# Weight splits of the next stage tied behind the norm's reciprocal root, and more slots for the squares, in a two-layer trunk

## The chip, the cores and the metric

One core of one Trainium2 chip runs the whole program. The metric is the device time of one execution in microseconds (us), taken as the median of several runs. The profile is of one execution of its own.

## The reference

A sequence of 512 tokens with 16 learned tokens ahead of it (528 rows of 1024 features) goes through an input norm and two layers. All of it is in fp32. Cut to what matters here:

```python
for l in range(DEPTH):                       # DEPTH = 2
    h = layer_norm(DEEPNORM_ALPHA * h + 0.5 * swiglu_ffn(h, ffn1_w13[l], ffn1_w2[l]), ln_g[l, 0], ln_b[l, 0])
    mix = token_mix(h, w_in[l], ...)         # pooled, convolved and retention groups, one projection in, one out
    h = layer_norm(DEEPNORM_ALPHA * h + mix, ln_g[l, 1], ln_b[l, 1])
    h = layer_norm(DEEPNORM_ALPHA * h + 0.5 * swiglu_ffn(h, ffn2_w13[l], ffn2_w2[l]), ln_g[l, 2], ln_b[l, 2])
return h[:, N_META:]

def swiglu_ffn(x, w13, w2):
    a, u = jnp.split(x @ w13, 2, axis=-1)
    return (jax.nn.silu(a) * u) @ w2
```

`layer_norm` takes the mean and the variance over the 1024 features, and multiplies by the reciprocal root of the variance.

## The kernel before

**Stages.** The stages follow each other as f0a, m0, f0b, f1a, m1, f1b: ffn, mixer, ffn of layer 0, then of layer 1. After each of the first five stands a norm, after the last another form of it. So there are five places where a norm of this kind leads over to the first products of the next stage: f0a to m0, m0 to f0b, f0b to f1a, f1a to m1, m1 to f1b.

**Tiles.** Features lie on the partitions: the activations are eight tiles (m = 0 to 7) of 128 features, in two halves s of the tokens, 264 columns each. A matmul in full precision is three products of rounded parts (`mm3`, L130): high by high, low by high, high by low. So each operand is split in two: `weights()` (L86) has SP load a weight of 128x1024 into a "raw" tile (4 buffers), ScalarE casts it to its high part (L91), and VectorE subtracts that in two pieces of 512 columns to get the low part (L94).

**The norm.** `center` (L273) adds up the tiles and takes their mean by a matmul with ones (L283). VectorE subtracts the mean from each tile (L289), and ScalarE squares each (L291) into tiles q0 to q7 of the tag "q", which has 4 buffers. POOL adds q1 to q3 onto q0 and VectorE adds q5 to q7 onto q4 (both L296); VectorE joins the two sums (L298). `inv_var` (L182) sums the squares per token by small matmuls (L189), then a chain of eleven tiny VectorE operations on 88x3 elements (`inv_root`, L161 to L172) makes the reciprocal root, and a last one sets it on a diagonal (L192, the tile dg). Its instruction is kept in `rooted`. `inv_spread` (L201) spreads the diagonal over the partitions by a matmul, and `norm_apply` (L304) scales each tile (L308) and splits it into its x parts, high (L312, L315 on ScalarE) and low (even m on VectorE, L318 or L320; odd m on POOL, L313).

**Order around the norm.** `normed` (L337) issues the last step of the stage for the first half, that half's statistics, then the second half's steps for the same tiles, and the second half's statistics. The roots of the halves are `rooted["first"]` and `rooted["second"]`. A scheduler of the language orders each engine's instructions by its own estimate of when they are ready; `tc.issue_after(ins)` makes what is traced in its block follow `ins` on the engine of `ins`, here VectorE, and on no other.

**The next stage's first weights.** In an ffn, `hidden_part` (L488) takes three units in the plain way (0, 1 and 21); units 0 and 1 have two weights each, 21 one. In the mixer, the loop at L580 loads four weights for the "u" group (w0, w2, then w1, w3) and two for "xp" (w4, w5). Of these, only unit 21's splits are tied, behind the second root. Later ffn weights are sums of blocks, split by other functions (L431).

Of the kernel before, what the change touches and what calls it, by code (L numbers as in the profile page):

```python
# [40 lines left out]
PACE = (4, 3, 3, 2, 0)  # L41

ON_POOL = ("f0a_0", "f0a_1", "f0a_21")
LATE, LATE_W, LATE_B = 3, 2, 2

HM = NM // 2
NT = 256 + HM
# [11 lines left out]
def trunk(ctx, tc, a):  # L59
# [16 lines left out]
    def raw(r):  # L76
        return r.bitcast(F32)
# [5 lines left out]
        return vec[lo:hi, j : j + 1]  # L83


    def weights(src, n, name, e=nc.vector):  # L86
        w = wp.tile([P, 1024], F32, tag="raw", name=f"{name}_r", bufs=RAW)
        hi = wp.tile([P, 1024], F32R, tag="hi", name=f"{name}_h", bufs=WB)
        lo = wp.tile([P, 1024], F32R, tag="lo", name=f"{name}_l", bufs=WB)
        nc.sync.dma_start(out=w[:, :n], in_=src)  # L90
        nc.scalar.copy(out=hi[:, :n], in_=w[:, :n])  # L91
        for c in range(0, n, 512):
            sl = slice(c, min(c + 512, n))
            e.tensor_tensor(out=lo[:, sl], in0=w[:, sl], in1=raw(hi[:, sl]), op=ALU.subtract)  # L94
        return hi, lo

    def weights_wide(src, n, name):
# [175 lines left out]
    def center(tiles, n, width, name):  # L273

        s = tiles[0]
        if len(tiles) > 1:
            s = t(f"{name}_s", "s")
            nc.gpsimd.tensor_tensor(out=s[:, :n], in0=tiles[0][:, :n], in1=tiles[1][:, :n], op=ALU.add)  # L278
            for i, y in enumerate(tiles[2:]):
                e = nc.vector if i == len(tiles) - 3 else nc.gpsimd  # L280
                e.tensor_tensor(out=s[:, :n], in0=s[:, :n], in1=y[:, :n], op=ALU.add)  # L281
        mean = stat(f"{name}_mean")
        nc.tensor.matmul(mean[:, :n], lhsT=ones[width], rhs=s[:, :n], start=True, stop=True)  # L283

# [12 lines left out]
        if early:
            nc.vector.tensor_tensor(out=ss[0][:, :n], in0=ss[0][:, :n], in1=ss[1][:, :n], op=ALU.add)  # L298
        return inv_spread(inv_var(ss[0], n, width, name), n, name)
# [188 lines left out]
    def hidden_part(part, src, ns, name, between={}):  # L488
        hid, w = {}, {}
        plain = PARTS[part][: AHEAD if part == 0 else 0]  # L490
        for u, s in in_two(plain, AHEAD, between):
            if s == 0:
                i = plain.index(u)
                late = "first" in rooted and i >= LATE_W
                with tc.issue_after(rooted["second" if i >= LATE_B else "first"]) if late else nullcontext():
                    w[u] = unit_weights(u, src, f"{name}_{u}")
                hid[u] = []
            hid[u].append(hidden(u, w[u], s, ns[s], f"{name}_{u}"))
        if part == 0:
            summed[name] = sums(ns[0], name)  # L500
        for u in PARTS[part][len(plain) :]:
            with tc.issue_after(rooted["second"]) if plain and "second" in rooted else nullcontext():
                wu = sum_weights(src["p"][u], f"{name}_{u}")
            hid[u] = hidden_by_sums(wu, summed[name], ns[0], f"{name}_{u}")
        return hid
# [60 lines left out]
    def mixer(l, name):  # L566
# [13 lines left out]
        for (kind, c), s in in_two([("u", 0), ("u", 1), ("xp", 0), ("xp", 1)], 3):  # L580
            n = ns[s]
            if s == 0:
                tiles = (c, 2 + c) if kind == "u" else (4 + c,)
                ws[kind, c] = [weights(w_in[i], 1024, f"{name}w{i}") for i in tiles]
                p_ = pad if kind == "u" else ppad
                seq[kind, c] = wide(f"{name}{kind}{c}")[:, : p_ + L]
                nc.gpsimd.memset(seq[kind, c][:, :p_], 0.0)  # L587
            ps = project(ws[kind, c], s, n, f"{name}p{kind}{c}{s}")
            x_ = seq[kind, c]
            if kind == "u":  # L590
                sg = t(f"{name}sg{c}{s}", "g")
# [482 lines left out]
```

## Time and profile before

| | us |
|---|---|
| median of 3 runs (lowest, highest) | 1979.4 (1978.49, 1981.81) |
| the profiled execution, own time | 1979.3 |
| its span | 1977.5 |
| mean granted clock of TensorE | 0.99 |

The profile's rows use PE for TensorE's matmuls, DVE for VectorE, ACT for ScalarE, POOL for GpSimd and SP for the queue that loads weights. Numbers of buffers and halves are left out of names, so `f0a_ln_q` is any of the squares of the norm behind f0a. A row of a timeline has its start in us from the span's start, its length, the engine, the line and operation, what it writes and reads, the count, and in brackets how long the engine stood idle before it and what ended that. Lengths of one engine's instructions overlap a little, so the step from one start to the next is what an instruction costs in a row of them.

### The profile page before, as it was taken

Reading aid. Unit: us, or ns where it says so; the run is one execution under the profiler, and the core shown is the slowest. Engines: PE = TensorE matmul, PEld = TensorE weight load, DVE = VectorE, ACT = ScalarE, POOL = GpSimd, SP = SyncE. Lnnn points to the kernel's source line nnn. Section 1 sums busy time; section 2 is a strip of 40 time slices with the busy share of each in tenths; the row PEclk is TensorE's granted clock in tenths of the full one; section 3 lists DMA queues with packets and bytes.
Section 4 is the critical chain, followed back from the end, with each engine's and each line's share of the span. In section 5 each row is a group of like instructions: output and inputs, shape, how many; then the busy total and the mean of one; then the engine's idle time right before and its main releaser. Section 6 shows DMA issues by size and latency. Waiting matters only on the chain.

```text
span 1977.5 us, 36739 instructions
## 1 busy us (share of the span) xinstructions
PE 1912.4 (97%) x14423; PEld 1826.3 (92%) x14423; DVE 1548.9 (78%) x3466; ACT 920.1 (47%) x1845; POOL 215.0 (11%) x283
## 2 busy tenths in 40 slices
PE   7999999999999999999999999999999999999996
PEld 6999999997899899999989999998889998999995
DVE  7788778689767977788697787787897697877787
ACT  5454446443333644454464554464343265544451
POOL 4000000442003000000120000005320130000001
PEclk9999999999999999999999999999999999999998
DMA  4422323322112233323213323332131213323321
GB/s 143 129 86 97 116 88 104 100 76 85 63 34 75 64 98 108 97 89 107 95 54 111 101 89 107 97 118 75 65 104 54 65 44 118 107 86 107 107 97 43
DMA packets 61069, 177.98 MB, mean 90 GB/s; under 512 B 6976, under 2 KB 10944, under 8 KB 60896
## 3 DMA queue, kind: packets, MB, share of 16 engines
q1 hardware_dynamic: 59744, 174.59, 27.8%
q8 instruction: 113, 1.85, 0.4%
q10 hardware_dynamic: 1152, 1.05, 0.2%
q14 instruction: 60, 0.49, 0.1%
HBM read 173.52 MB, written 2.10 MB: 89 GB/s over the span
## 4 chain that ended last, share of the span: by engine, by line
PE 79%; DVE 12%; POOL 3%; issue 3%; ACT 2%; DMA 0%; SPq 0%; DVEq 0%; POOLq 0%; ACTq 0%
PE f0a_y L134 2%; PE f0a_y L133 2%; PE f1bo L890 2%; PE f1bo L888 2%; PE f0a_y L135 2%; PE f1bo L889 2%; PE f0b_y L134 2%; PE f1a_y L134 2%; PE f0b_y L133 2%; PE f0b_y L135 2%; PE f1a_y L135 2%; PE f1a_y L133 2%; DVE m0y L610 1%; DVE m1y L610 1%; PE m0sc L719 1%
## 5 line engine op out<-in xcount | busy, mean ns | idle before, releaser
L610 DVE SCALAR_TENSOR_TENSOR m1y<-m1u,vec,m1y 128x528 f32<-128x528 f32 x60 | 46.1, 801 | 0.0
L91 ACT CAST f0a_o_h<-f0a_o_r 128x512 fp32r<-128x512 f32 (+1 forms) x37 | 23.5, 635 | 48.4 <-PE f0a_y L134 29.5
L610 DVE SCALAR_TENSOR_TENSOR m0y<-m0u,vec,m0y 128x528 f32<-128x528 f32 x60 | 45.9, 801 | 0.0
L91 ACT CAST f1a_o_h<-f1a_o_r 128x512 fp32r<-128x512 f32 (+1 forms) x37 | 23.6, 637 | 48.0 <-PE f1a_y L134 29.0
L91 ACT CAST f0b_o_h<-f0b_o_r 128x512 fp32r<-128x512 f32 (+1 forms) x37 | 23.5, 636 | 47.6 <-PE f0b_y L134 29.3
L335 DVE TENSOR_TENSOR x<-x,f0a_y 128x264 f32<-128x264 f32 x64 | 27.1, 425 | 23.3 <-PE f0a_y L135 23.1
L335 DVE TENSOR_TENSOR h<-h,f0b_y 128x264 f32<-128x264 f32 x64 | 27.1, 425 | 23.2 <-PE f0b_y L135 23.1
L335 DVE TENSOR_TENSOR h<-h,f1a_y 128x264 f32<-128x264 f32 x64 | 27.1, 424 | 23.1 <-PE f1a_y L135 23.0
L94 DVE TENSOR_TENSOR f1bw_l<-f1bw_r,f1bw_h 128x512 fp32r<-128x512 f32 x42 | 27.7, 688 | 17.6 <-ACT f1bw_h L91 17.0
L949 POOL TENSOR_TENSOR yt<-yt,g_last 128x256 f32<-128x256 f32 x4 | 3.0, 740 | 337.2 <-ACT yt L948 337.2
L94 DVE TENSOR_TENSOR f0a_o_l<-f0a_o_r,f0a_o_h 128x512 fp32r<-128x512 f32 (+1 forms) x42 | 26.6, 642 | 13.4 <-ACT f0a_o_h L91 11.3
L94 DVE TENSOR_TENSOR f1a_o_l<-f1a_o_r,f1a_o_h 128x512 fp32r<-128x512 f32 (+1 forms) x42 | 26.7, 642 | 13.4 <-ACT f1a_o_h L91 11.4
L94 DVE TENSOR_TENSOR f0b_o_l<-f0b_o_r,f0b_o_h 128x512 fp32r<-128x512 f32 (+1 forms) x42 | 26.7, 642 | 12.6 <-ACT f0b_o_h L91 10.4
L278 POOL TENSOR_TENSOR f0b_ln_s<-h,h 128x264 f32<-128x264 f32 x2 | 1.6, 820 | 313.8 <-DVE h L335 313.8
L587 POOL MEMSET m1u<- 128x30 f32 x2 | 0.2, 123 | 307.6 <-PE f1a_20Q L135 307.6
L587 POOL MEMSET m0u<- 128x30 f32 x2 | 0.2, 123 | 306.1 <-PE f0a_20Q L135 306.1
L91 ACT CAST f1bw_h<-f1bw_r 128x1024 fp32r<-128x1024 f32 (+1 forms) x22 | 22.2, 1011 | 21.0 <-PE f1bo L890 4.2
L894 DVE TENSOR_TENSOR yt<-yt,f1bo 128x256 f32<-128x256 f32 x80 | 27.8, 414 | 5.4 <-PE f1bo L890 5.3
L291 ACT ACTIVATE m_ln_q<-h 128x264 f32<-128x264 f32 (+1 forms) x32 | 11.9, 414 | 39.7 <-DVE h L289 36.1
L257 PE MATMUL tr<-ident,xtok 128*128 128x128 f32 (+1 forms) x48 | 10.9, 328 | 12.1 <-DVE xtok L242 11.4
L281 POOL TENSOR_TENSOR m_ln_s<-m_ln_s,h 128x264 f32<-128x264 f32 (+1 forms) x20 | 18.2, 912 | 32.0 <-DVE h L329 26.1
L257 PEld LDWEIGHTS tr<-ident,xtok 128*128 128x128 f32 (+1 forms) x48 | 6.8, 167 | 16.1 <-issue 14.8
(10805 smaller groups left out, 9335.0 us busy)
## 6 DMA issues: line engine op xcount, KB each, us to landing
f1bw_r<-in_w2last SPq DMA_DIRECT2D x20, 512.0 KB, 3.8
f0a_o_r<-in_w SPq DMA_DIRECT2D x32, 256.0 KB, 2.7
f0b_o_r<-in_w SPq DMA_DIRECT2D x32, 256.0 KB, 2.8
f1a_o_r<-in_w SPq DMA_DIRECT2D x32, 256.0 KB, 2.9
m0wo_r<-in_w_out SPq DMA_DIRECT2D x8, 512.0 KB, 3.5
m1wo_r<-in_w_out SPq DMA_DIRECT2D x8, 512.0 KB, 3.5
m0w_r<-in_w_in SPq DMA_DIRECT2D x6, 512.0 KB, 4.4
m1w_r<-in_w_in SPq DMA_DIRECT2D x6, 512.0 KB, 4.3
```

The lines of the kernel that those rows point to most:

```text
L91: nc.scalar.copy(out=hi[:, :n], in_=w[:, :n])
L94: e.tensor_tensor(out=lo[:, sl], in0=w[:, sl], in1=raw(hi[:, sl]), op=ALU.subtract)
L133: nc.tensor.matmul(out, lhsT=wh, rhs=xh, start=start, stop=False, skip_group_check=onto)
L134: nc.tensor.matmul(out, lhsT=wh, rhs=xl, start=False, stop=False, skip_group_check=onto)
L135: nc.tensor.matmul(out, lhsT=wl, rhs=xh, start=False, stop=stop, skip_group_check=onto)
L335: nc.vector.tensor_tensor(out=y, in0=y, in1=ps, op=ALU.add)
L610: nc.vector.scalar_tensor_tensor(out=ys[c], in0=src, scalar=wk, in1=ys[c], op0=ALU.mult, op1=ALU.add)
L719: nc.tensor.matmul(sc[:kn, :cw], lhsT=kk[ks][:, kc : kc + kn], rhs=qq[s][:, c0 : c0 + cw], start=True, stop=True)
L888: nc.tensor.matmul(o, lhsT=hh, rhs=wh, start=part > 0 and i == 0, stop=False)
L889: nc.tensor.matmul(o, lhsT=hh, rhs=wl, start=False, stop=False)
L890: nc.tensor.matmul(o, lhsT=hl, rhs=wh, start=False, stop=i == nk - 1)
L894: nc.vector.tensor_tensor(out=y[:, :256], in0=y[:, :256], in1=o, op=ALU.add)
```

## The change

`LATE_W` goes. A helper `hold()` puts `issue_after` around the cast and the splits of `weights()`, behind the instruction that `held["by"]` names at that time. In an ffn it is the first root for units 0 and 1, the second root for unit 21. In the mixer it is the first root for the four "u" weights, the second for the two "xp" weights. The tie holds VectorE's splits; casts are ScalarE's and loads are SP's, and keep their place by the scheduler's estimates. f0a has no norm of this kind ahead of it and is not touched. In norms of eight tiles, the squares with odd numbers take their tile from the tag "sm" (5 buffers), which other stages use too, so that the eight squares of a norm draw on 9 buffers in place of 4. No instruction is added or removed, and SP's loads keep their order.

```diff
--- before.py
+++ after.py
@@ -41,7 +41,7 @@
 PACE = (4, 3, 3, 2, 0)
 
 ON_POOL = ("f0a_0", "f0a_1", "f0a_21")
-LATE, LATE_W, LATE_B = 3, 2, 2
+LATE, LATE_B = 3, 2
 
 HM = NM // 2
 NT = 256 + HM
@@ -83,15 +83,22 @@
         return vec[lo:hi, j : j + 1]
 
 
+    held = {"by": None}
+
+    def hold():
+
+        return tc.issue_after(held["by"]) if held["by"] is not None else nullcontext()
+
     def weights(src, n, name, e=nc.vector):
         w = wp.tile([P, 1024], F32, tag="raw", name=f"{name}_r", bufs=RAW)
         hi = wp.tile([P, 1024], F32R, tag="hi", name=f"{name}_h", bufs=WB)
         lo = wp.tile([P, 1024], F32R, tag="lo", name=f"{name}_l", bufs=WB)
         nc.sync.dma_start(out=w[:, :n], in_=src)
-        nc.scalar.copy(out=hi[:, :n], in_=w[:, :n])
-        for c in range(0, n, 512):
-            sl = slice(c, min(c + 512, n))
-            e.tensor_tensor(out=lo[:, sl], in0=w[:, sl], in1=raw(hi[:, sl]), op=ALU.subtract)
+        with hold():
+            nc.scalar.copy(out=hi[:, :n], in_=w[:, :n])
+            for c in range(0, n, 512):
+                sl = slice(c, min(c + 512, n))
+                e.tensor_tensor(out=lo[:, sl], in0=w[:, sl], in1=raw(hi[:, sl]), op=ALU.subtract)
         return hi, lo
 
     def weights_wide(src, n, name):
@@ -287,7 +294,7 @@
         ss, q = [], []
         for i, y in enumerate(tiles):
             nc.vector.tensor_tensor(out=y[:, :n], in0=y[:, :n], in1=mean[:, :n], op=ALU.subtract)
-            q.append(t(f"{name}_q{i}", "q"))
+            q.append(t(f"{name}_q{i}", "sm" if k > 2 and i % 2 else "q"))
             nc.scalar.activation(q[i][:, :n], y[:, :n], AF.Square)
             if i == early or i == 0:
                 ss.append(q[i])
@@ -491,9 +498,10 @@
         for u, s in in_two(plain, AHEAD, between):
             if s == 0:
                 i = plain.index(u)
-                late = "first" in rooted and i >= LATE_W
-                with tc.issue_after(rooted["second" if i >= LATE_B else "first"]) if late else nullcontext():
-                    w[u] = unit_weights(u, src, f"{name}_{u}")
+                late = part == 0 and "first" in rooted
+                held["by"] = rooted["second" if i >= LATE_B else "first"] if late else None
+                w[u] = unit_weights(u, src, f"{name}_{u}")
+                held["by"] = None
                 hid[u] = []
             hid[u].append(hidden(u, w[u], s, ns[s], f"{name}_{u}"))
         if part == 0:
@@ -581,7 +589,9 @@
             n = ns[s]
             if s == 0:
                 tiles = (c, 2 + c) if kind == "u" else (4 + c,)
+                held["by"] = rooted["first" if kind == "u" else "second"]
                 ws[kind, c] = [weights(w_in[i], 1024, f"{name}w{i}") for i in tiles]
+                held["by"] = None
                 p_ = pad if kind == "u" else ppad
                 seq[kind, c] = wide(f"{name}{kind}{c}")[:, : p_ + L]
                 nc.gpsimd.memset(seq[kind, c][:, :p_], 0.0)
```

What the change moves is shown on two engines for the first of the five places. Line numbers after are higher by 7 in these functions (L94 is L101, L133 to L135 are L140 to L142, L192 is L199, L296 is L303, L308 is L315).

On VectorE, from the first half's last add of squares on, before (m0w is a mixer weight, x with its number the half's tile, f0a_y the product that it takes in):

```order
L296 TENSOR_TENSOR f0a_ln_q_4783<-f0a_ln_q_4783,f0a_ln_q_4794 128x264
L94 TENSOR_TENSOR m0w_l<-m0w_r,m0w_h 128x512
L298 TENSOR_TENSOR f0a_ln_q_4768<-f0a_ln_q_4768,f0a_ln_q_4783 128x264
L335 TENSOR_TENSOR x_3_1_493<-x_3_1_493,f0a_y_3_1_4893 128x264
L161 TENSOR_SCALAR f0a_ln_v<-f0a_ln_rs 88x3
L94 TENSOR_TENSOR m0w_l<-m0w_r,m0w_h 128x512
L162 TENSOR_SCALAR f0a_ln_y<-f0a_ln_v,bits 88x3
L94 TENSOR_TENSOR m0w_l<-m0w_r,m0w_h 128x512
L167 SCALAR_TENSOR_TENSOR f0a_ln_g<-f0a_ln_y,f0a_ln_v 88x3
L335 TENSOR_TENSOR x_4_1_503<-x_4_1_503,f0a_y_4_1_4910 128x264
L169 SCALAR_TENSOR_TENSOR f0a_ln_w<-f0a_ln_g,f0a_ln_y 88x3
L94 TENSOR_TENSOR m0w_l<-m0w_r,m0w_h 128x512
```

and after, to the first scaling of the norm:

```order
L303 TENSOR_TENSOR f0a_ln_q_4783<-f0a_ln_q_4783,f0a_ln_q_4794 128x264
L305 TENSOR_TENSOR f0a_ln_q_4768<-f0a_ln_q_4768,f0a_ln_q_4783 128x264
L168 TENSOR_SCALAR f0a_ln_v<-f0a_ln_rs 88x3
L342 TENSOR_TENSOR x_3_1_493<-x_3_1_493,f0a_y_3_1_4893 128x264
L169 TENSOR_SCALAR f0a_ln_y<-f0a_ln_v,bits 88x3
...
L177 SCALAR_TENSOR_TENSOR f0a_ln_y<-f0a_ln_w,f0a_ln_y 88x3
L342 TENSOR_TENSOR x_4_1_503<-x_4_1_503,f0a_y_4_1_4910 128x264
L199 SCALAR_TENSOR_TENSOR f0a_ln_dg<-ident,f0a_ln_y 88x264
L101 TENSOR_TENSOR m0w_l<-m0w_r,m0w_h 128x512 x2
L315 SCALAR_TENSOR_TENSOR x_0_0_155<-x_0_0_155,vec,f0a_ln_rs 128x264
```

The splits L94 that stood between the adds and inside the chain have left this part, except two of one weight, which follow the diagonal (L199).

On VectorE in the second half, behind the subtracts of the mean, before:

```order
L289 TENSOR_TENSOR x_7_1_533<-x_7_1_533,f0a_ln_mean 128x264
L296 TENSOR_TENSOR f0a_ln_q_5004<-f0a_ln_q_5004,f0a_ln_q_5007 128x264
L320 SCALAR_TENSOR_TENSOR f0a_ln_x4l<-x_4_0_195,vec,f0a_ln_x4h 128x264
L296 TENSOR_TENSOR f0a_ln_q_5004<-f0a_ln_q_5004,f0a_ln_q_5011 128x264
L308 SCALAR_TENSOR_TENSOR x_6_0_215<-x_6_0_215,vec,f0a_ln_rs 128x264
L296 TENSOR_TENSOR f0a_ln_q_5004<-f0a_ln_q_5004,f0a_ln_q_5015 128x264
L308 SCALAR_TENSOR_TENSOR x_7_0_225<-x_7_0_225,vec,f0a_ln_rs 128x264
L298 TENSOR_TENSOR f0a_ln_q_4989<-f0a_ln_q_4989,f0a_ln_q_5004 128x264
L320 SCALAR_TENSOR_TENSOR f0a_ln_x6l<-x_6_0_215,vec,f0a_ln_x6h 128x264
L161 TENSOR_SCALAR f0a_ln_v<-f0a_ln_rs 88x3
L94 TENSOR_TENSOR m0w_l<-m0w_r,m0w_h 128x512
```

and after:

```order
L296 TENSOR_TENSOR x_7_1_533<-x_7_1_533,f0a_ln_mean 128x264
L303 TENSOR_TENSOR f0a_ln_q_5004<-f0a_ln_q_5004,f0a_ln_q_5007 128x264
L327 SCALAR_TENSOR_TENSOR f0a_ln_x6l<-x_6_0_215,vec,f0a_ln_x6h 128x264
L303 TENSOR_TENSOR f0a_ln_q_5004<-f0a_ln_q_5004,f0a_ln_q_5011 128x264
L101 TENSOR_TENSOR m0w_l<-m0w_r,m0w_h 128x512
L303 TENSOR_TENSOR f0a_ln_q_5004<-f0a_ln_q_5004,f0a_ln_q_5015 128x264
L101 TENSOR_TENSOR m0w_l<-m0w_r,m0w_h 128x512
L305 TENSOR_TENSOR f0a_ln_q_4989<-f0a_ln_q_4989,f0a_ln_q_5004 128x264
L101 TENSOR_TENSOR m0w_l<-m0w_r,m0w_h 128x512
L168 TENSOR_SCALAR f0a_ln_v<-f0a_ln_rs 88x3
L101 TENSOR_TENSOR m0w_l<-m0w_r,m0w_h 128x512
L169 TENSOR_SCALAR f0a_ln_y<-f0a_ln_v,bits 88x3
```

Six of the splits now alternate with the second half's adds and its chain; x6's low part stands behind the first add, where it stood behind the joining one.

On PE, the mixer's first products, before (m0w0 to m0w3 are the four "u" weights, `_h` and `_l` their high and low parts, x0h and x0l the parts of x0):

```order
L133 MATMUL m0pu00_0_5128<-f0a_ln0_x0h_4821,m0w0_h_5113 128x264
L133 MATMUL m0pu00_1_5129<-f0a_ln0_x0h_4821,m0w2_h_5120 128x264
L133 MATMUL m0pu10_0_5198<-f0a_ln0_x0h_4821,m0w1_h_5183 128x264
L134 MATMUL m0pu00_0_5128<-f0a_ln0_x0l_4822,m0w0_h_5113 128x264
L135 MATMUL m0pu00_0_5128<-f0a_ln0_x0h_4821,m0w0_l_5114 128x264
L134 MATMUL m0pu00_1_5129<-f0a_ln0_x0l_4822,m0w2_h_5120 128x264
L135 MATMUL m0pu00_1_5129<-f0a_ln0_x0h_4821,m0w2_l_5121 128x264
L133 MATMUL m0pu00_0_5128<-f0a_ln0_x1h_4826,m0w0_h_5113 128x264
L134 MATMUL m0pu00_0_5128<-f0a_ln0_x1l_4827,m0w0_h_5113 128x264
L135 MATMUL m0pu00_0_5128<-f0a_ln0_x1h_4826,m0w0_l_5114 128x264
```

and after, from the first product on, and further on where x6 comes in:

```order
L140 MATMUL m0pu00_0_5128<-f0a_ln0_x0h_4821,m0w0_h_5113 128x264
L141 MATMUL m0pu00_0_5128<-f0a_ln0_x0l_4822,m0w0_h_5113 128x264
L142 MATMUL m0pu00_0_5128<-f0a_ln0_x0h_4821,m0w0_l_5114 128x264
L140 MATMUL m0pu00_1_5129<-f0a_ln0_x0h_4821,m0w2_h_5120 128x264
L141 MATMUL m0pu00_1_5129<-f0a_ln0_x0l_4822,m0w2_h_5120 128x264
L140 MATMUL m0pu00_0_5128<-f0a_ln0_x1h_4826,m0w0_h_5113 128x264
L141 MATMUL m0pu00_0_5128<-f0a_ln0_x1l_4827,m0w0_h_5113 128x264
...
L140 MATMUL m0pu00_0_5128<-f0a_ln0_x6h_5053,m0w0_h_5113 128x264
L140 MATMUL m0pu10_0_5198<-f0a_ln0_x0h_4821,m0w1_h_5183 128x264
L141 MATMUL m0pu10_0_5198<-f0a_ln0_x0l_4822,m0w1_h_5183 128x264
L140 MATMUL m0pu10_1_5199<-f0a_ln0_x0h_4821,m0w3_h_5190 128x264
L141 MATMUL m0pu10_1_5199<-f0a_ln0_x0l_4822,m0w3_h_5190 128x264
```

Before, products by several weights alternate tile by tile. After, the first weight goes through x0 to x6 by itself, with the other weights' low parts behind it.

## Rows read from the trace of the kernel before

**Rows 1.** The page: busy us (share) of each engine with instructions; a DMA's KB and us.

```profile
PE 1912.4 (97%) x14423; PEld 1826.3 (92%) x14423; DVE 1548.9 (78%) x3466; ACT 920.1 (47%) x1845; POOL 215.0 (11%) x283
...
m0w_r<-in_w_in SPq DMA_DIRECT2D x6, 512.0 KB, 4.4
```

**Rows 2.** PE's list of waits over the span: total us, times, longest.

```profile
PE f1b_2Q L133 <- ACT f1b_2x_hi L415: 3.1, 1, 3.1
...
PE f1a_2P L135 <- DVE f1a_2a_lo L431: 2.5, 1, 2.5
...
PE f1a_ln_rs L189 <- DVE f1a_ln_q L298: 1.8, 1, 1.8
...
PE m_ln_rs L189 <- DVE m_ln_q L298: 1.6, 2, 0.9
```

**Rows 3.** Timeline of ACT, first transition: start, length, instruction, [idle before].

```profile
374.45 0.43 ACT L291 ACTIVATE f0a_ln_q<-x 128x264 f32<-128x264 f32 x1 [0.40 <-POOL f0a_ln_q L296]
374.79 1.03 ACT L91 CAST m0w_h<-m0w_r 128x1024 fp32r<-128x1024 f32 x1
375.72 0.42 ACT L291 ACTIVATE f0a_ln_q<-x 128x264 f32<-128x264 f32 x1
```

**Rows 4.** Timeline of DVE, first transition, first half's norm.

```profile
376.17 0.95 DVE L296 TENSOR_TENSOR f0a_ln_q<-f0a_ln_q,f0a_ln_q 128x264 f32<-128x264 f32 x1 [0.44 <-ACT f0a_ln_q L291]
377.05 0.68 DVE L94 TENSOR_TENSOR m0w_l<-m0w_r,m0w_h 128x512 fp32r<-128x512 f32 x1
377.65 0.42 DVE L298 TENSOR_TENSOR f0a_ln_q<-f0a_ln_q,f0a_ln_q 128x264 f32<-128x264 f32 x1
...
378.79 0.16 DVE L161 TENSOR_SCALAR f0a_ln_v<-f0a_ln_rs 88x3 f32<-88x3 f32 x1 [0.38 <-PE f0a_ln_rs L189]
...
385.87 0.42 DVE L192 SCALAR_TENSOR_TENSOR f0a_ln_dg<-ident,f0a_ln_y 88x264 f32<-88x264 f32 x1
...
387.56 1.29 DVE L308 SCALAR_TENSOR_TENSOR x<-x,vec,f0a_ln_rs 128x264 f32<-128x264 f32 x3 [0.60 <-PE f0a_ln_rs L201]
```

**Rows 5.** Timeline of DVE, first transition, second half's norm.

```profile
395.60 0.64 DVE L296 TENSOR_TENSOR f0a_ln_q<-f0a_ln_q,f0a_ln_q 128x264 f32<-128x264 f32 x1 [0.60 <-ACT f0a_ln_q L291]
...
400.58 0.28 DVE L162 TENSOR_SCALAR f0a_ln_y<-f0a_ln_v,bits 88x3 int32<-88x3 int32 x1
...
402.38 0.43 DVE L192 SCALAR_TENSOR_TENSOR f0a_ln_dg<-ident,f0a_ln_y 88x264 f32<-88x264 f32 x1
```

**Rows 6.** Timeline of POOL, first transition and f0b to f1a.

```profile
372.00 2.42 POOL L296 TENSOR_TENSOR f0a_ln_q<-f0a_ln_q,f0a_ln_q 128x264 f32<-128x264 f32 x3 [4.53 <-ACT f0a_ln_q L291]
...
991.11 3.99 POOL L281 TENSOR_TENSOR f0b_ln_s<-f0b_ln_s,h 128x264 f32<-128x264 f32 x1 [1.89 <-DVE f0b_ln_w L169]
```

**Rows 7.** Busy us by stretch: PE, PEld, DVE, ACT, POOL, then granted clock, DMA.

```profile
379.70:383.10 3.40, 3.40 (x18) 3.40 (x17) 3.34 (x10) 0.00 (x0) 1.14 (x1) 0.50 0.46 160
1035.06:1038.50 3.44, 3.44 (x18) 3.44 (x17) 2.31 (x4) 1.79 (x4) 0.00 (x0) 0.50 0.02 5
1639.20:1646.00 6.80, 5.72 (x25) 5.43 (x26) 6.73 (x13) 4.07 (x6) 0.00 (x0) 0.50 0.24 66
```

**Rows 8.** Timeline of PE, first transition.

```profile
386.92 0.61 PE L201 MATMUL f0a_ln_rs<-f0a_ln_dg,ones 88*128 88x264 f32 x2
...
388.66 0.63 PE L133 MATMUL m0pu<-f0a_ln_x0h,m0w_h 128*128 128x264 f32 x3 [0.89 <-ACT f0a_ln_x0h L315]
```

**Rows 9.** Timeline of PE, f1a to m1.

```profile
1364.93 0.71 PE L201 MATMUL f1a_ln_rs<-f1a_ln_dg,ones 88*128 88x264 f32 x2 [0.65 <-DVE f1a_ln_dg L192]
```

**Rows 10.** Timeline of DVE, f0b to f1a.

```profile
988.78 0.98 DVE L94 TENSOR_TENSOR f1a_0a_l<-f1a_0a_r,f1a_0a_h 128x512 fp32r<-128x512 f32 x1
...
994.40 0.72 DVE L170 SCALAR_TENSOR_TENSOR f0b_ln_y<-f0b_ln_w,f0b_ln_y 88x3 f32<-88x3 f32 x1
...
1007.71 0.16 DVE L161 TENSOR_SCALAR f0b_ln_v<-f0b_ln_rs 88x3 f32<-88x3 f32 x1 [0.58 <-PE f0b_ln_rs L189]
...
1011.40 0.88 DVE L308 SCALAR_TENSOR_TENSOR h<-h,vec,f0b_ln_rs 128x264 f32<-128x264 f32 x2
```

## The prediction

> **What bounds the kernel now.** The page's busy times come first: PE is busy for 1912.4 us of the span, in 14,423 matmuls, so 0.133 us is the mean of one [rows 1]. About 65 us of PE idleness is all that a reordering can reach, apart from the clock. The profiled execution took 1979.3 us, the median of the three runs is 1979.4, so the sum is made against 1979.3 and stands for the median too.
>
> The waits of PE say where the idleness is [rows 2]. The ones near the change are the row sums of the squares (L189) waiting for the last add of the squares: 1.8 us in each of the three norms that end an ffn (f0a, f0b and f1a; one row shown), 0.9 at most in the two that end a mixer. Farther behind, the first products of a later unit of the ffn (its weights are sums, hence f1a_2P and f1b_2Q) wait for a weight's split: 2.5 us in f1a, 3.1 in f1b. So some 7 us stand in front of L189.
>
> The ScalarE rows of the first transition (f0a to the mixer m0) tell why [rows 3]. A square is a step of 0.34 (374.45 to 374.79). From the fifth on, three of them wait 0.24, 0.41 and 0.40, together 1.05, for POOL's adds to free a slot (the last of the three is shown). The eighth starts only at 375.72, behind a cast of a weight, a step of 0.93. On VectorE [rows 4] a split of 512 columns (L94, a step of 0.60, from 377.05 to 377.65) stands between the last two adds, and eight more stand inside the reciprocal root, whose eleven small steps take from 378.79 (L161) to 385.87 (L192): 7.1 us. In the second half of the same norm the steps follow each other without a split from 400.58 to 402.38, 1.8 us [rows 5].
>
> **The squares and the chain, first transition (A).** Without the slot waits and the cast, the eighth square starts at 375.72 − 1.05 − 0.93 = 373.7 and is done by 374.1 instead of 376.1. POOL's three adds end at 374.4 [rows 6], and VectorE's add that joins the two sums cannot start before. One split of 0.60 in front of it is gone too. It would start at 374.5 at best; the adds on VectorE stretch beside POOL, 0.95 where 0.42 is usual [rows 4], so I take 375.2 to 376.0 instead of 377.65. L189 then has no wait or one of at most 0.7, and the root follows uninterrupted: L161 at about 377, L192 at 379.3 to 379.9, six microseconds earlier than before.
>
> PE cannot use six. Between L189 and L201 it works on the last products of f0a. Its idle before L189 is 1.8, and a stretch of 3.40 us right behind it ran at a granted clock of 0.50, the lower of the two levels [rows 7], which cost 1.7. With both gone, L201 moves from 386.92 to about 383.4, limited by PE, and the first mixer product from 388.66 to 385.2 [rows 8]: **3.5 earlier**, up to 4.1 if the 0.89 wait before it shrinks by 0.6 because PE has more of f0a left.
>
> **What is given back.** The nine splits are not gone: they stand behind the root now, all but two of them in or after the second half's norm, as the rows of VectorE's order show. PE begins the mixer with one of four weights split. It has the first weight against x0 to x5 and x6's high part (19 products) and six products of x0 by the other weights' high parts, 25 at 0.133: 3.3 us, plus waits for the x tiles as they come. Then it needs x6's low part, which VectorE issues behind all eight second-half subtracts and their first add. (Before, it stood behind their last add, but PE had all four weights against x0 to x5 to work through meanwhile.) Before, the first add came 8.0 us after the first scaling (387.56 to 395.60) [rows 4, 5]; counted from a first scaling at 384.1 it comes at 392.1, x6's low part at 393.0, while PE stands from about 390.7. That is a **new wait of 2.3**, and one of 0.6 at x7; two small waits of together 0.5 in the same stretch go. Given back: 2.4, or 1.7 if the second-half subtracts come sooner. A nets −1.1 to −2.4. I take −1.6, nearer the lower gain, because the splits now stand beside POOL's adds of the second norm. The mixer behind it is PE's own work, so what is left is kept.
>
> Splits that come later also free the raw buffers later. The mixer's fifth weight takes the first one's, so its load, 4.4 us from issue to landing [rows 1], starts when the first weight is split: at about 381 now, and it lands by 386. Its own products stand behind those of four weights in both halves, 2 × 4 × 24 of 0.133 or 25 us behind the first one at 385.2. That covers it, and a load would cost something only from 20 us of lateness on.
>
> **The same at f1a to m1 (D).** No half clock was there before. The gain in front of L201 is the 1.8 wait [rows 2] plus the 0.65 wait for the diagonal [rows 9]: 2.45, up to 3.05 with the same 0.6. Less 1.7 to 2.4 given back: between 0 and −1.4. I take −0.8.
>
> **f0b to f1a (B).** Here VectorE is the limit: some 23 us behind the norm, just ahead of the stretch at 1035.06 [rows 7], PE waits 2.5 us for a split that VectorE makes [rows 2]. So VectorE's time up to the second half's scaling counts (1011.40, with one split of 0.60 still owed) [rows 10]. What goes: 0.4 of waiting for the last square, 0.5 by which the last add is stretched beside POOL as in A, 0.9 by which a split (0.98) and a step of the root (0.72, where 0.15 is usual) are stretched, and about 1.6 of gaps in the second root (0.6 in front of it, 1.0 inside), filled by splits. What comes: the gaps of the first root, bare now, 0.8, or up to 1.9 if the splits stretch beside POOL in their new place. So 3.4 less 0.8 to 1.9: −1.5 to −2.6. I take −1.9, near the lower gain for the same reason as in A.
>
> On the stretching: one POOL add in B took 3.99 us [rows 6], where three took 2.42 in A, while a train of splits ran on VectorE. The Trainium skill, "SBUF — State Buffer", section "Who interferes with whom", says that a VectorE operation with two SBUF inputs and a GpSimd operation that reads SBUF exclude each other for the whole instruction. The rows agree with it. By it all that the first root wins would come back as blocking in the second half, where three POOL adds of squares now meet four splits; that is the second rival below.
>
> **Mixer to ffn (C, E).** L189 waits 0.9 at most, and the first weight's two splits, which VectorE made in slack ahead of the norm, now stand behind the root: 2 × 0.60 = 1.2 more in a tight stretch. 0.9 against part of 1.2: −0.4 to +0.3 each, taken as 0.
>
> **The clock.** The 2.5 wait in f1a and the 3.1 in f1b were each followed by a granted clock of 0.50 (1035.06 for 3.44 us, 1639.20 for 6.80) [rows 2, 7]; of the three waits of 1.8 before L189, one was (A). The new waits of 2.3 in A and D could go either way. A stretch of 3.4 us costs 1.7; at even odds in both places that is 1.7, and about half of it falls where PE waits for splits anyway: +0.8.
>
> **Sum.** −1.6 − 1.9 − 0.8 + 0 + 0 + 0.8 = −3.5: 1979.3 − 3.5 = **1975.8 us**. A measurement of this kernel can tell about 0.2%, 4.0 us, from no change, so the forecast lies just inside "the same".
>
> **Rivals.** (1) *Full gain*: no clock loss, no stretching beside POOL: A −2.4, B −2.6, D −1.4, C and E −0.4 each: −7.2, 1972. For it speaks that the 1.0 of slot waits is saved in the second half as well; against it, that splits and POOL's adds do meet. (2) *The wait only moves*: what L189 no longer waits, PE waits at x6 and for the other three weights; A and D net 0 after a half-clock stretch each, B gives back what POOL blocks: 0 ± 2, 1979. For it speak the single split weight and VectorE as the limit in B; against it, that the bare chain takes 1.8 us where it took 7.1 [rows 4, 5]. (3) *Slower by the clock*: PE's wait for x6 brings a stretch of 6.8 us at the lower level, as the 3.1 wait in f1b did. Each costs 3.4. In A and D alone that is +6.8 against the −4.3 of A, B and D, so +2.5: still the same. It decides from three places on, A, B and D: 10.2 − 4.3 = +5.9, 1985. For it speaks that x6's low part stands behind the second-half subtracts in all three; against it, that VectorE and not PE is the limit in B, and that no wait of 2.3 has yet been seen to bring the long stretch.
>
> **Chances.** The forecast (−6 to −1): 0.43. Full gain (below −6): 0.16. Only moved (−1 to +4): 0.28. Slower by the clock (above +4): 0.13. Faster than −4.0 are full gain and a good half of the forecast: 0.40. Slower than +4.0 is the clock rival: 0.13. The same holds 0.47. The range for 8 in 10 reaches from part of full gain, 1970.5, to the edge of the clock rival, 1982.5; the forecast's own is 1973 to 1978.
>
> **What would show it.** In the profile after: squares in A without slot waits and the last one done near 374; L189's waits gone from the list of waits (below 0.7 each), L161 to L192 under 3 us in the first half; no granted clock of 0.50 near 380. Against that, a wait of PE of about 2 us at x6's low part in A and D. In B, the split that f1a waits for should come about 2 earlier. It is wrong if L189 still waits over 1 us (POOL's adds set it), if the x6 wait is far from 2.3, if new half-clock stretches stand behind it, or if the mixer-to-ffn transitions move by over 1 us.

## The result and the profile after

The changed kernel takes 1994.16 us, the median of 4 runs (1988.43 to 1995.18), against 1978.95 for the kernel before in the same comparison: a ratio of 1.0068, with a 95% interval of 1.0056 to 1.008. It is **slower by 0.7%**, about 15 us, where 3.5 us less were forecast. The range ended at 1982.5; the side that came true was given 0.13. The profiled execution took 1995.18 us over a span of 1993.4, 15.9 more than before.

The page's busy times, and then PE's list of waits (total, times, longest), of the changed kernel:

```profile
PE 1919.4 (96%) x14423; PEld 1833.3 (92%) x14423; DVE 1554.0 (78%) x3466; ACT 917.2 (46%) x1845; POOL 210.0 (11%) x283
```

```profile
PE m0pu L141 <- DVE f0a_ln_x6l L327: 2.9, 1, 2.9
PE m1pu L141 <- DVE f1a_ln_x6l L327: 2.9, 1, 2.9
PE f1a_0p L141 <- DVE f0b_ln_x4l L325: 2.6, 2, 2.3
PE m_ln_mean L290 <- DVE m_ln_s L288: 2.5, 2, 1.8
...
PE f1a_ln_rs L196 <- DVE f1a_ln_q L305: 0.8, 1, 0.8
```

The matmuls are the same 14,423, and PE is busy 7 us longer with them [rows 1]: no work was added, and the mean granted clock is 0.985 where it was 0.99. The wait before the row sums (L189, now L196) fell from 1.8 to 0.8 or 0.9 behind each ffn (one row shown) [rows 2]. In its place stand waits for x6's and x4's low parts and for the second half's mean (L290).

To see where the 15.9 us arise, I took the same PE instructions in both traces as marks: the first mean of each norm, the last product of a mixer's first group and so on, and compared the time from mark to mark. A is f0a to m0, C m0 to f0b, B f0b to f1a, D f1a to m1, E m1 to f1b; m0 and m1 are what lies inside the mixers behind their first products. Each number is one profiled execution less the one of before, in us; the rest of the program adds 0.3 to the changed kernel. The changed kernel and the one with the second units tied run the same instructions ahead of A, and yet that part is +0.1 in one trace and −1.6 in the other. So a small entry by itself is weak evidence.

| kernel | A | m0 | C | B | D | m1 | E |
|---|---|---|---|---|---|---|---|
| changed | +4.1 | +1.1 | +2.8 | −0.3 | +4.6 | +1.9 | +1.4 |
| changed, PE's wait filled | +0.5 | −0.2 | +1.3 | −0.3 | +1.1 | +0.9 | −0.5 |
| changed, x4 to x7 first | −1.5 | −1.0 | +2.4 | +2.9 | +0.5 | +0.1 | +1.1 |
| ties in the ffns alone | −1.2 | −1.2 | +2.2 | +1.7 | −1.3 | −0.2 | +0.9 |
| ties in the mixers alone | +3.8 | −0.6 | +0.4 | −0.3 | +4.7 | −0.4 | −0.4 |
| ties alone, four slots | +2.9 | −1.2 | +3.6 | +1.2 | +4.2 | +0.9 | +0.7 |
| slots alone | −1.0 | +0.1 | −0.1 | −0.7 | +0.5 | +0.1 | +0.5 |
| second units tied | −2.3 | −1.2 | +0.3 | +0.4 | −1.9 | +1.0 | +1.3 |
| second units tied, mixers alone | −2.5 | −1.0 | −1.1 | −0.7 | −2.0 | −0.1 | +3.8 |
| ties in the mixers alone, PE's wait filled | +0.5 | +0.9 | −0.8 | −0.3 | +1.1 | +1.1 | +0.7 |

More than half of the loss is in A and D, where a gain had been forecast. The timeline of ScalarE and of VectorE in A shows that the first half of the norm does what was expected:

```profile
371.55 2.31 ACT L298 ACTIVATE f0a_ln_q<-x 128x264 f32<-128x264 f32 x7
```

```profile
375.85 0.79 DVE L305 TENSOR_TENSOR f0a_ln_q<-f0a_ln_q,f0a_ln_q 128x264 f32<-128x264 f32 x1
377.36 0.16 DVE L168 TENSOR_SCALAR f0a_ln_v<-f0a_ln_rs 88x3 f32<-88x3 f32 x1 [0.72 <-PE f0a_ln_rs L196]
...
380.50 0.42 DVE L199 SCALAR_TENSOR_TENSOR f0a_ln_dg<-ident,f0a_ln_y 88x264 f32<-88x264 f32 x1
...
389.67 2.79 DVE L296 TENSOR_TENSOR x<-x,f0a_ln_mean 128x264 f32<-128x264 f32 x8
392.38 0.48 DVE L303 TENSOR_TENSOR f0a_ln_q<-f0a_ln_q,f0a_ln_q 128x264 f32<-128x264 f32 x1
392.78 0.97 DVE L327 SCALAR_TENSOR_TENSOR f0a_ln_x6l<-x,vec,f0a_ln_x6h 128x264 fp32r<-128x264 f32 x1
```

Seven squares run without a wait and end at 373.86, the sums are joined at 375.85 instead of 377.65, and the root takes 3.1 us (377.36 to 380.50) instead of 7.1 [rows 4]. PE starts the mixer 2.6 us earlier than before, at 386.04 instead of 388.66 [rows 8]. Then x6's low part comes behind the eight subtracts, and PE's timeline and the busy times by stretch (granted clock in the third column from the end) show what follows:

```profile
386.04 0.29 PE L140 MATMUL m0pu<-f0a_ln_x0h,m0w_h 128*128 128x264 f32 x1
...
390.48 0.29 PE L140 MATMUL m0pu<-f0a_ln_x0h,m0w_h 128*128 128x264 f32 x1
390.60 0.28 PE L141 MATMUL m0pu<-f0a_ln_x0l,m0w_h 128*128 128x264 f32 x1
393.81 0.59 PE L141 MATMUL m0pu<-f0a_ln_x6l,m0w_h 128*128 128x264 f32 x1 [2.92 <-DVE f0a_ln_x6l L327]
394.19 0.42 PE L142 MATMUL m0pu<-f0a_ln_x6h,m0w_l 128*128 128x264 f32 x1
394.41 0.42 PE L140 MATMUL m0pu<-f0a_ln_x7h,m0w_h 128*128 128x264 f32 x1
```

```profile
393.20:403.44 10.24, 9.61 (x43) 9.30 (x44) 8.34 (x25) 1.70 (x3) 2.44 (x5) 0.50 0.40 114
482.00:488.83 6.83, 5.93 (x26) 5.23 (x24) 5.55 (x12) 0.39 (x1) 2.35 (x2) 0.50 0.37 122
673.10:679.93 6.83, 5.99 (x27) 5.99 (x28) 4.87 (x10) 3.31 (x6) 0.00 (x0) 0.50 0.00 1
1011.00:1014.41 3.41, 3.41 (x15) 3.32 (x16) 3.41 (x6) 0.66 (x2) 1.82 (x2) 0.51 0.22 41
1379.70:1389.94 10.24, 9.37 (x42) 9.07 (x43) 8.34 (x25) 1.93 (x3) 2.67 (x5) 0.50 0.41 112
1468.40:1475.23 6.83, 6.17 (x27) 5.29 (x25) 5.67 (x12) 0.38 (x1) 4.30 (x2) 0.50 0.20 56
1652.70:1656.11 3.41, 2.85 (x13) 2.86 (x14) 2.73 (x5) 0.48 (x2) 0.00 (x0) 0.51 0.00 0
```

A product takes the step 0.12 before the wait (390.48 to 390.60) and 0.22 behind it (394.19 to 394.41): PE stands 2.92 us and then works at the lower of the two levels for 10.24 us. These are all the stretches at 0.50 but the one at the program's end, 47.8 us together. Before, there were three of [rows 7] and three more, with the same columns:

```profile
475.30:482.13 6.83, 5.90 (x22) 4.86 (x23) 6.83 (x16) 2.03 (x3) 2.81 (x3) 0.50 0.26 79
666.40:669.81 3.41, 3.40 (x15) 3.41 (x16) 2.19 (x4) 0.75 (x2) 0.00 (x0) 0.50 0.00 0
1454.90:1458.31 3.41, 3.41 (x14) 3.06 (x14) 3.41 (x9) 0.55 (x1) 1.60 (x1) 0.50 0.29 120
```

They sum to 27.3. So 20.5 us more ran at half the clock: up to 10.2 us of the 15.9, if PE had work all the time. By place, A has 10.24 where 3.41 stood before, D 10.24 where none stood, C and m1 6.83 for 3.41 each, E 3.41 less; m0 and B have as much as before.

### The profile page after: what moved, and what is told of

It reads as the page before. It is cut to its first block, busy times and chain, and to the rows that moved or that the text cites. A ratio compares the mean times of both kernels' runs of the same rounds, so it can differ in the third digit from the quotient of the medians.

```text
span 1993.4 us, 36725 instructions
## 1 busy us (share of the span) xinstructions
PE 1919.4 (96%) x14423; PEld 1833.3 (92%) x14423; DVE 1554.0 (78%) x3466; ACT 917.2 (46%) x1845; POOL 210.0 (11%) x283
## 4 chain that ended last, share of the span: by engine, by line
PE 78%; DVE 14%; issue 3%; ACT 2%; POOL 1%; DMA 1%; SPq 0%; DVEq 0%; ACTq 0%; POOLq 0%
PE f1bo L900 2%; PE f1bo L898 2%; PE f1bo L899 2%; PE f0a_y L141 2%; PE f0b_y L141 2%; PE f1a_y L141 2%; PE f0b_y L142 2%; PE f0a_y L142 2%; PE f0b_y L140 2%; PE f0a_y L140 2%; PE f1a_y L142 2%; PE f1a_y L140 2%; DVE m1y L620 1%; DVE m0y L620 1%; PE m1o L748 1%
## 5 line engine op out<-in xcount | busy, mean ns | idle before, releaser
L342 DVE TENSOR_TENSOR h<-h,f0b_y 128x264 f32<-128x264 f32 x64 | 27.3, 426 | 23.4 <-PE f0b_y L142 23.2
L342 DVE TENSOR_TENSOR x<-x,f0a_y 128x264 f32<-128x264 f32 x64 | 27.3, 426 | 23.3 <-PE f0a_y L142 23.1
L342 DVE TENSOR_TENSOR h<-h,f1a_y 128x264 f32<-128x264 f32 x64 | 27.3, 426 | 23.2 <-PE f1a_y L142 23.0
L101 DVE TENSOR_TENSOR f1bw_l<-f1bw_r,f1bw_h 128x512 fp32r<-128x512 f32 x42 | 27.8, 688 | 18.2 <-ACT f1bw_h L98 17.7
L101 DVE TENSOR_TENSOR f1a_o_l<-f1a_o_r,f1a_o_h 128x512 fp32r<-128x512 f32 (+1 forms) x42 | 26.6, 642 | 14.1 <-ACT f1a_o_h L98 12.0
L101 DVE TENSOR_TENSOR f0a_o_l<-f0a_o_r,f0a_o_h 128x512 fp32r<-128x512 f32 (+1 forms) x42 | 26.7, 643 | 13.3 <-ACT f0a_o_h L98 11.4
L101 DVE TENSOR_TENSOR f0b_o_l<-f0b_o_r,f0b_o_h 128x512 fp32r<-128x512 f32 (+1 forms) x42 | 26.7, 642 | 12.7 <-ACT f0b_o_h L98 10.6
L141 PE MATMUL m0mo<-m0cat,m0wo_h 128*128 128x264 f32 x64 | 18.6, 292 | 0.0
```

The lines of the kernel that those rows point to most:

```text
L141: nc.tensor.matmul(out, lhsT=wh, rhs=xl, start=False, stop=False, skip_group_check=onto)
L342: nc.vector.tensor_tensor(out=y, in0=y, in1=ps, op=ALU.add)
```

## The experiments

The theory after the result: PE gets only one split weight in time, runs out of work before x6, and the clock falls behind that wait. The rival: the order as such costs, because splits behind the root come late wherever PE needs them, and the low clock falls into time that is lost anyway.

**PE's wait filled.** 24 products that nobody reads give PE work for the 2.9 us in both mixers; the order of everything else stays:

```diff
+            if k == 6 and fill:
+                idle = acc(f"{name}_idle", "att")
+                wh, xh = at(ws[0], slice(5 * P, 6 * P))[0], xs[5][s][0]
+                for j in range(fill):
+                    nc.tensor.matmul(idle[:, :n], lhsT=wh, rhs=xh[:, :n], start=True, stop=True)
 ...
-            ps = project(ws[kind, c], s, n, f"{name}p{kind}{c}{s}")
+            ps = project(ws[kind, c], s, n, f"{name}p{kind}{c}{s}", 24 if (kind, c, s) == ("u", 0, 0) else 0)
```

> The changed kernel with 24 more products (x5's high part by the first weight's high part, into a bank that nobody reads) ahead of x6 in the first product group of each mixer, so that PE works through the 2.9 us in which it waited for x6's low part; nothing else moves. Theory (the clock): the granted clock stays at 1.00 behind that place, where it stood at 0.50 for 10.24 us in both mixers, so that each mixer starts about 5 us earlier: 1994 - 10 = 1984, 1983 to 1987. Rival (the order): PE is held up by weights that are split late, and the low clock only falls into time that is lost anyway: 1992 to 1996.

Measured: 1984.6 us, ratio 1.0026 (1.0013 to 1.0039), against 1.0068 for the change. PE's timeline and the same two stretches as above:

```profile
390.02 3.09 PE L381 MATMUL m0pu_idle<-f0a_ln_x5h,m0w_h 128*128 128x264 f32 x24
...
393.76 0.39 PE L141 MATMUL m0pu<-f0a_ln_x6l,m0w_h 128*128 128x264 f32 x1
```

```profile
393.20:403.44 10.24, 9.81 (x77) 9.14 (x76) 9.90 (x29) 2.08 (x4) 2.40 (x5) 1.00 0.48 153
1379.70:1389.94 10.24, 10.24 (x85) 10.17 (x84) 7.85 (x21) 5.83 (x15) 5.66 (x20) 1.00 0.41 133
```

The product by x6's low part starts at the same time as in the changed kernel, 393.76 against 393.81, but PE does 77 matmuls in the 10.24 us behind it instead of 43. A drops from +4.1 to +0.5 and D from +4.6 to +1.1. That the low clock comes behind this wait is shown, and its price is 3.6 and 3.5 us in the two places, where the expectation had about 5 in each. The median is in the theory's range because the rest fell too: the two traces differ by 13.6 us, of which A and D are 7.1, and the medians by 9.6. The rival keeps what is left: at the full clock A and D are no gain over the kernel before, and the slots alone give more in both (−1.0 and +0.5).

**x4 to x7 first.** The low part of x6 is brought ahead of the subtracts.

```diff
+        norm_apply(0, ns[0], ra, v, range(4, KT), f"{name}0", keep)
         rb = norm_stats(1, ns[1], f"{name}1")
         rooted["second"] = rooted["last"]
-        norm_apply(0, ns[0], ra, v, range(4, KT), f"{name}0", keep)
```

> The changed kernel with the scaling and the splits of x4 to x7 of the first half issued ahead of the second half's statistics, so that x6's low part stands before the eight subtracts on VectorE. Theory (the clock, brought by the wait for x6): the 2.9 us waits and the 10.24 us stretches at 0.50 go in both mixers, at a price of about 1 us of later statistics each: 1994 - 12 = 1982, 1978 to 1984. Rival (the order): PE waits for the three weights' splits instead, the waits move to their low parts and the sum stays: 1989 to 1995.

Measured: 1985.99 us, ratio 1.0033 (1.0023 to 1.0043), above the theory's range and below the rival's. The mixers went as the theory has it (A −1.5, D +0.5). The ffns pay: B is 3.1 worse than in the changed kernel. There PE waits 3.6 us for a later unit's split, with 6.83 us at 0.50 behind it (1035.00 to 1041.83); before, it was 2.5 with 3.41. The rival has a part in A too. PE's timeline there:

```profile
394.90 0.39 PE L142 MATMUL m0pu<-f0a_ln_x4h,m0w_l 128*128 128x264 f32 x1 [2.02 <-DVE m0w_l L101]
```

PE waits 2.02 for another weight's low part; the granted clock stayed at 1.00 from 385 to 410.

**The parts of the change.** The slots alone, the ties alone, and the ties at the ffns or at the mixers alone:

```diff
 # slots alone, on the kernel before
-            q.append(t(f"{name}_q{i}", "q"))
+            q.append(t(f"{name}_q{i}", "sm" if k > 2 and i % 2 else "q"))
 # ties alone, on the changed kernel: the same line back to "q"
 # ties in the ffns alone, on the changed kernel
-                held["by"] = rooted["first" if kind == "u" else "second"]
 # ties in the mixers alone, on the changed kernel
-                late = part == 0 and "first" in rooted
+                late = part == 0 and "first" in rooted and i >= LATE_B
```

> The kernel before with the more slots for the squares alone, no ties. Theory: the ties make the loss and the slots a small gain; the wait of 1.8 us before the row sums shrinks by about 1 us after each ffn, and the chain with the splits in it follows as before: 1975 to 1979. Rival: the slots do part of the harm, since squares that no longer wait push casts and adds together: 1981 to 1985.

Measured: 1976.26 us, ratio 0.9983 (0.9974 to 0.9993). The slots are a gain of about 3 us by themselves, and the wait before the row sums fell from 1.8 to 1.0 in A, B and D.

> The changed kernel with the squares in four slots as before: the ties alone. Theory (the ties' loss and the slots' gain add up): the changed kernel's 1994 plus the 3 us that the slots gave by themselves, 1994 to 1999. Rival (the slots make the loss worse, since a first half that ends earlier waits longer for x6): 1988 to 1993.

Measured: 1992.11 us, ratio 1.0069 (1.0054 to 1.0084): in the rival's range, but not for its reason. The wait for x6 is no shorter than in the changed kernel, 3.06 against 2.92; the stretch behind it is. PE's row, and the stretch with what follows it:

```profile
394.19 0.55 PE L141 MATMUL m0pu<-f0a_ln_x6l,m0w_h 128*128 128x264 f32 x1 [3.06 <-DVE f0a_ln_x6l L327]
```

```profile
394.30:397.71 3.41, 3.41 (x14) 3.09 (x15) 3.23 (x6) 1.51 (x2) 2.33 (x4) 0.51 0.09 10
397.71:404.50 6.79, 6.79 (x58) 6.72 (x58) 5.76 (x21) 0.57 (x2) 0.00 (x0) 1.00 0.72 218
```

In A there is a second stretch, behind the row sums as in the kernel before, so that A has 6.83 us at 0.50 in all, against 10.24 with the slots:

```profile
377.19:380.60 3.41, 3.41 (x17) 3.41 (x17) 2.55 (x12) 0.00 (x0) 0.75 (x1) 0.50 0.02 5
```

With or without the slots the ties cost 0.7%. Whether the slots' 3 us come on top of that is left open, since the two intervals leave room for it. In A, the slots end the stretch behind the row sums, and the one behind x6 is 6.83 longer with them: +4.1 with the slots, +2.9 without.

> The changed kernel without the ties of the mixer's weights; the ties of the ffn's first weights and the slots stay. Theory: the losses at f0a to m0 (4.1), in m0 (1.1), at f1a to m1 (4.5) and in m1 (1.9) go, those at m0 to f0b (2.8) and m1 to f1b (1.3) stay: 1979 + 4 = 1983, 1980 to 1986. Rival (all ties cost alike, wherever they are): 1987 to 1991.

Measured: 1980.9 us, ratio 1.001 (1.0 to 1.0019), the theory's range. C and E stay 2.2 and 0.9 above before, and A and D are as with the slots alone or better. B is +1.7, where the changed kernel has −0.3; 6.83 us at 0.50 stand in it instead of 3.41.

> The changed kernel with the ties of the mixers' weights and none on the ffns' units 0 and 1, the slots as in the change. Theory (each place pays for itself): the wait of 2.9 us at x6 and the stretch of 10.24 us in both mixers as in the changed kernel, and none of the losses at m0 to f0b and m1 to f1b: the slots alone at 1976 plus 5.5 and 6 of the mixers and about 2 inside them, 1986 to 1991. Rival (the ffn's ties make most of it): 1978 to 1983.

Measured: 1987.76 us, ratio 1.0061 (1.0037 to 1.0084), the theory's range: A +3.8 and D +4.7, each again with 10.24 us at 0.50, and C, B and E within 0.5 of before. The mixers' ties make most of the loss. The five times spread widely, from 1984.76 to 1996.72.

**The mixers' ties, with the wait filled.** The two edits together (ties in the mixers alone, 24 products).

> The kernel with the mixers' ties alone and the slots (1988 measured), with the 24 idle products ahead of x6 in each mixer. Theory (the clock): without the wait no stretch at 0.50 in either place, 3.5 to 5 us less at each: 1978 to 1981; what stays above the slots alone (1976) is the wait's own time, now filled with work that nobody needs. Rival (the order): 1985 to 1990.

Measured: 1979.63 us, ratio 0.9997 (0.9986 to 1.0008), the theory's range, 8.1 us below the kernel without the filling. It confirms the clock's part a second time: neither place has a stretch at 0.50, A goes from +3.8 to +0.5 and D from +4.7 to +1.1.

**Second units tied.** The first weights stay untied, so that PE has two split ones.

```diff
-                held["by"] = rooted["first" if kind == "u" else "second"]
+                held["by"] = None if (kind, c) == ("u", 0) else rooted["first" if kind == "u" else "second"]
-                late = part == 0 and "first" in rooted
+                late = part == 0 and "first" in rooted and i >= 1
```

> The changed kernel with the first unit's two weights left untied (unit 0 in an ffn, w0 and w2 in a mixer); the ties of the rest and the slots stay. Theory (PE with one split weight runs out of work before x6, and the clock falls behind that wait): with two weights split PE has the work, no wait of over 1 us at x6 and no 10.24 us stretch in either mixer, and the second half's mean is not late at m0 to f0b: about as with the slots alone, 1975 to 1980. Rival (any split behind the root comes back as a wait in the second half): half of the loss stays, 1984 to 1989.

Measured: 1977.81 us, ratio 0.9989 (0.9978 to 0.9999), the theory's range. PE's wait for x6 in A:

```profile
393.38 0.39 PE L141 MATMUL m0pu<-f0a_ln_x6l,m0w_h 128*128 128x264 f32 x1 [0.60 <-DVE f0a_ln_x6l L327]
```

0.60 instead of 2.92, no stretch at 0.50 in A or D, and A and D at −2.3 and −1.9: here the earlier root is a gain in these two places. C is +0.3 instead of +2.8. In the whole time nothing is left of it: the slots alone (0.9983) are as fast.

**Second units tied in the mixers alone.** The first of those two lines, with the ffns as before the change.

> The slots, and in the mixers the ties on w1, w3, w4 and w5 alone; w0 and w2 untied, and the ffns' units 0 and 1 untied as before the change. Theory (ties help where PE keeps two split weights to work with, and cost where VectorE is the limit): by place, the gains that the trace with the second unit tied showed at the two mixers (about 2 each) and those of the slots alone at the ffns: 1973 to 1976, below both kernels. Rival (the ties give nothing, the slots all): 1976 to 1978, as with the slots alone.

Measured: 1975.77 us, ratio 0.9976 (0.9963 to 0.999): the theory's range, below both kernels. Against the slots alone (0.9983) the intervals overlap, so whether these ties add anything is not told apart by the runs. The trace has A at −2.5 and D at −2.0, and E at +3.8, with a stretch of 6.83 us at 0.50 that no other trace has:

```profile
1658.03:1664.86 6.83, 6.83 (x27) 6.15 (x27) 0.00 (x0) 2.44 (x8) 0.00 (x0) 0.50 0.58 196
```

## Why the prediction was wrong

**The squares and the chain: right, and a little late.** The eighth square was to end at 374.1 and ended at 373.86; the sums were to be joined at 375.2 to 376.0 and were at 375.85; the wait before the row sums was to be at most 0.7 and is 0.8; the diagonal was to come at 379.3 to 379.9 and came at 380.50, with two adds of the stage's last step (L342) inside the root. L201 (now L208) was to come 3.5 earlier, held by PE; PE took it in between the last products of f0a, at 380.98, 5.9 earlier. The first mixer product was to come 3.5 earlier as well and came 2.6 earlier: 0.8 of the wait before the row sums stayed, and a wait of 0.6 stands before L208.

**The new wait for x6: right in place, a little small.** PE was to stand from 390.7 to 393.0. It stood from 390.9 to 393.81: VectorE's split of x6 took 0.97 where such a split takes 0.48 by itself (x6's in the trace of before). The 0.6 at x7 did not come.

**The clock: the step that failed.** The prediction said that the new waits in A and D "could go either way", took a stretch of 3.4 us at even odds, and called half of its price covered: +0.8 for both places. In the changed kernel both waits were followed by 10.24 us at 0.50, and filling the wait gave back 3.6 and 3.5 us: 7.1 where 0.8 had been put. The third rival had the mechanism, with a stretch of 6.8 in A, B and D; it came as 10.24 in A and D. In B, 3.41 us stand behind a new wait of 2.26 for x4's low part, and the 3.41 of before, behind the later split, are gone.

**What the ties earn without the clock: mis-sized.** A and D were to give −1.6 and −0.8. With the wait filled they are +0.5 and +1.1. The start of the mixer 2.6 us earlier does not pay for 2.9 us that PE spends on nothing. The slots alone give A −1.0 and D +0.5, so beside them the ties lose 1.5 and 0.6 at the full clock.

**B: the size was off.** −1.9 was forecast, −0.3 measured, and −0.3 as well without the ffns' ties. VectorE's time from the first subtract to the second half's scaling, before and after (busy time of VectorE in the third busy column):

```profile
979.68:1011.40 31.72, 28.16 (x216) 26.32 (x215) 27.94 (x81) 18.00 (x39) 15.40 (x16) 1.00 0.20 67
```

```profile
987.70:1020.73 33.03, 29.00 (x218) 27.87 (x217) 30.32 (x82) 17.68 (x39) 14.74 (x16) 0.95 0.18 55
```

The time rose by 1.3. One split more lies in it (0.6, the one that was owed). Idle time fell by 1.1 (31.72 − 27.94 = 3.8, now 33.03 − 30.32 = 2.7). But busy time rose by 2.4, of which that split is 0.6: the other 1.8 are the same operations made longer. The timeline of VectorE shows which:

```profile
1009.95 0.97 DVE L325 TENSOR_TENSOR f0b_ln_x4l<-h,f0b_ln_x4h 128x264 fp32r<-128x264 f32 x1
1010.84 0.97 DVE L303 TENSOR_TENSOR f0b_ln_q<-f0b_ln_q,f0b_ln_q 128x264 f32<-128x264 f32 x1
...
1012.34 0.98 DVE L303 TENSOR_TENSOR f0b_ln_q<-f0b_ln_q,f0b_ln_q 128x264 f32<-128x264 f32 x1
```

They take 0.97 where 0.42 is usual [rows 4], while POOL adds the last of the second half's squares and splits x5 and x7:

```profile
1009.82 0.81 POOL L303 TENSOR_TENSOR f0b_ln_q<-f0b_ln_q,f0b_ln_q 128x264 f32<-128x264 f32 x1
1010.59 0.93 POOL L320 TENSOR_TENSOR f0b_ln_x5l<-h,f0b_ln_x5h 128x264 fp32r<-128x264 f32 x1
1011.74 1.30 POOL L320 TENSOR_TENSOR f0b_ln_x7l<-h,f0b_ln_x7h 128x264 fp32r<-128x264 f32 x1 [0.21 <-ACT f0b_ln_x7h L319]
```

The prediction had 1.4 us of such lengthening go and at most 1.1 come anew; on balance 1.8 came, which is what the second rival had for B. The direction agrees with the Trainium skill, "SBUF — State Buffer", section "Who interferes with whom", by which a VectorE operation with two SBUF inputs and a GpSimd operation that reads SBUF shut each other out; which one held the other here was not tried.

**C and E: a wait that was not listed.** 0 was forecast, +2.8 and +1.4 measured. In C, PE waits 1.78 for the second half's mean (0.7 in E), and VectorE's rows say why:

```profile
639.94 0.71 PE L290 MATMUL m_ln_mean<-m_ln_s,ones 128*128 128x264 f32 x2 [1.78 <-DVE m_ln_s L288]
```

```profile
635.17 0.68 DVE L101 TENSOR_TENSOR f0b_0u_l<-f0b_0u_r,f0b_0u_h 128x512 fp32r<-128x512 f32 x1
...
637.41 0.99 DVE L336 SCALAR_TENSOR_TENSOR h<-f0a_ln_x7l,h 128x264 f32<-128x264 f32 x1
638.32 0.68 DVE L101 TENSOR_TENSOR f0b_0u_l<-f0b_0u_r,f0b_0u_h 128x512 fp32r<-128x512 f32 x1
638.92 0.96 DVE L288 TENSOR_TENSOR m_ln_s<-m_ln_s,h 128x264 f32<-128x264 f32 x1
```

The two splits of unit 0's second weight, which ran ahead of the root and inside it before, now stand among the residual of the last tile and the last add of the mean, and three operations there take 0.96 to 0.99. The prediction counted only the first weight's two splits and named nobody who waits for what is queued behind. With unit 0 untied, C is +0.3; with no ffn ties, C is +0.4 and E −0.4. The stretch at 673, 6.83 us where 3.41 stood before, accounts for up to 1.7 more: with PE's wait filled 3.41 us stand there again, and C is +1.3. E is not taken apart further.

**m0 and m1.** The prediction had the mixers keep what A and D win; +1.1 and +1.9 arise inside them, far behind the ties. They go with the length of the low stretch there. The changed kernel has 6.83 us in each (at 482.00 and 1468.40, above). The kernel with the ties in the ffns alone has 3.41 in each:

```profile
473.59:477.00 3.41, 2.99 (x9) 1.95 (x10) 3.41 (x9) 1.61 (x2) 1.72 (x2) 0.50 0.52 154
1453.21:1456.62 3.41, 3.36 (x11) 2.35 (x12) 3.41 (x9) 1.17 (x1) 1.61 (x1) 0.50 0.34 136
```

Over all the changed traces, m1 is +0.9 to +1.9 where 6.83 us stand in it and −0.4 to +0.1 with 3.41, as before, or none. m0, which had 6.83 before, is −0.2 to +1.1 with 6.83 and −1.2 to −0.6 with 3.41 or none. What makes the stretch there long or short was not tried.

**The sum.** Between the forecast of −3.5 and the trace's +15.9 lie 19.4 us: 6.3 of the clock in A and D, 4.0 of what the ties earn there without it, 1.6 of B, 4.2 of C and E, 3.0 of m0 and m1, and 0.3 elsewhere.

## What to carry to other kernels

Work that is taken off a chain does not leave: before moving it, ask which engine will stand where it lands, and for how long, and price that wait with the clock that follows it, not with its own length. When the next stage can start on one operand of several, keep as many of them ready as cover the time to the next dependence: tying the second pair and leaving the first pair free turned a loss of 0.7% into a time 0.1% to 0.2% below the kernel before, which is about what the slots give by themselves. And a sequence of two edits is best timed apart: here one was a gain of 0.2% that the other hid.

## What the runs showed of the hardware

A wait of PE of 2.92 us was followed by 10.24 us at a granted clock of 0.50 in the changed kernel, and one of 2.9 again with the mixers' ties alone; a wait of 3.06 was followed by 3.41 us with the ties alone, and a wait of 2.02 by none (A, with x4 to x7 first). Before, one wait of 1.8 was followed by 3.41 us and two others by none, and one of 3.1 by 6.83. And 6.83 us came with no wait of over 0.4 in the 20 us ahead of them (at 1658.03, second units tied in the mixers alone), behind the products named `f1btr`, which every kernel has and which no such stretch follows in the other traces. The length of the wait alone does not say whether a stretch comes or how long it is, and these runs don't settle what does. Work that nobody needs, 24 products in the place of the wait, kept the clock at 1.00 behind it in A and D, and the median fell by 9.6 us (1994.16 to 1984.6).
